# Attention probabilities moved into float32r tiles by a transfer before their transposes, with a reordered list of work for the attention stage

## The chip, the core and the metric

The kernel runs on one core of a Trainium2 chip. The metric is the device time in microseconds of one execution. The core has five engines that each work through their own instructions in order: TensorE (PE, matmuls and transposes), VectorE (DVE), ScalarE (ACT), GpSimd (POOL) and SyncE (SP), which here only issues transfers. Transfers are done by 16 DMA engines; SP, ACT and POOL each have a queue to issue them on. Engines wait for each other, and for transfers, through semaphores.

## The reference

A decoder trunk of two layers over 256 tokens of width 1024, in float32. Each layer is a SwiGLU FFN, a token mixer and a second FFN, each between RMS norms. The mixer of the first layer is a recurrent block, that of the second is attention with a forget gate. The change touches the attention alone:

```python
def forgetting_attention(xq, w_q, w_o, k, v, c):
    q = (xq @ w_q).reshape(Bn, S, N_HEADS, HEAD_DIM).transpose(0, 2, 1, 3) * (HEAD_DIM ** -0.5)
    for blk in range(S // Q_BLOCK):              # 2 blocks of 128 queries
        logits = einsum('bhqd,bhkd->bhqk', q[:, :, q0:end], k[:, :, :end])
        logits = logits + c[:, :, q0:end, None] - c[:, :, None, :end]
        logits = where(kpos[None, :] <= qpos[:, None], logits, -inf)
        p = softmax(logits, axis=-1)
        outs.append(einsum('bhqk,bhkd->bhqd', p, v[:, :, :end]))
    o = concatenate(outs, axis=2).transpose(0, 2, 1, 3).reshape(Bn, S, D_ATTN)
    return o @ w_o
```

There are 16 heads of 64. The first block of queries sees 128 keys, the second 256.

## The kernel before

**Tiles.** The 256 tokens are two tiles of 128, called tile 0 and tile 1 here (`t` in the code). Matmuls over weights are made at float32r speed with float32's accuracy: each weight block of 128x1024 is loaded by SP into a tile `raw` (ring of 5), ACT makes its upper part `whi` (L173), DVE the remainder `wlo` (L177), and `mm3` does three matmuls for each pair of operands: upper with upper (L183), upper with lower (L184), lower with upper (L185).

**Slots.** A weight block with the work on it is an item. One slot is one item's work for one tile: six matmuls of 128x512 in the attention stage, from `mm3`. Between slots, `tick` runs work that was put off by some slots (`defer`), such as the transposes of the q heads (L983) and of the next stage's inputs (L214).

**Order.** PE's instructions stand in the order in which the program writes them (`manual_schedule`). The other engines' order is made by the framework's scheduler, which knows the dependences and the parts marked as of high priority; once built it is fixed.

**The attention stage.** Its order of PE work is the list `ATT_ORDER`, read in L1367 to L1373. A `0` or `1` is the next slot of that tile: first eight for q (`attn_w_q`), then eight for the output product (`attn_w_o`, items 0 to 7, one for each 128 rows of W_o). Items 0 to 3 need the heads 0 to 7 of the attention's output, items 4 to 7 the heads 8 to 15. For tile 0 the last item's matmuls are made with its own slot, for tile 1 the last two items' are held back and made together in the last slot (`rows0=1`, `rows=2`). A letter with a tile's number is the next step of that kind of the tile's attention; groups are four heads for tile 0 (four groups, 0 to 3) and two heads for tile 1 (eight groups, 0 to 7), so that a group's probabilities are always 128x512:

- `l` (`logits`, L1097): logits of two groups at once, so every second `l` is empty: eight matmuls for tile 0 (128 keys), four for tile 1 (256 keys), into two banks. DVE adds the bias and takes the row's extreme (L1118) into a tile `pe` (ring of 3), makes the exponent's offset (L1122, L1123), ACT makes the exponentials with their row sums (L1125).
- `n` (`norm`, L1129): DVE's reciprocal of the row sums (L1131) and the product with them, in place in `pe` (L1132).
- `t` (`turn`, L1134): four transposes of `pe` on PE (L1138), in float32 with the float32 identity `ident`, and ACT's copy from the bank into `pT` (L1140, ring of 4).
- `v` (`values`, L1142): the products of `pT` with the values (L1152): four matmuls for each group. Behind the last group of each half of the heads, ACT and DVE write the upper and lower part of the output, `oh` (L1158) and `ol` (L1159), which are the left operands of the output product.

When a tile's output product is done, `enter` makes its row norm (ACT squares L205, POOL L198 and L200), adds it to the stream `h` (DVE L272, L285), and some slots later transposes `h` (L214) for the next FFN, whose left operands ACT (L223) and DVE (L222, L228) write.

**Elsewhere.** The FFN moves its hidden tile from float32 into a float32r tile `prr` by a transfer on SP's queue (L515), and transposes it as float32r with the float32r identity `identr` (L525). Its `prr` tiles, like several others, come from the tag `t1` of `hpool` (ring of 2).

Of the kernel before, what the change touches and what calls it, by code (L numbers as in the profile page):

```python
# [9 lines left out]
F32 = mybir.dt.float32  # L10
F32R = mybir.dt.float32r
# [5 lines left out]
P = 128  # L17
# [26 lines left out]
def trunk_kernel(ctx: ExitStack, tc: tile.TileContext, A: dict, out: bass.AP):  # L44
    nc = tc.nc
# [5 lines left out]
    hpool = ctx.enter_context(tc.tile_pool(name="h", bufs=1))  # L51
# [6 lines left out]
    def nm(s):  # L58
        uid[0] += 1
        return f"{s}_{uid[0]}"  # L60

    def mmbank():
        return psum.tile([P, 512], F32, tag="mm", name=nm("mm"), bufs=4)

    def gtbank():
        return psum.tile([P, 512], F32, tag="gt", name=nm("gt"), bufs=2)

    def trbank():
        return psum.tile([P, 512], F32, tag="tr", name=nm("tr"), bufs=2)
# [44 lines left out]
    ident = cpool.tile([P, P], F32, name="ident")  # L114
    make_identity(nc, ident)
    identr = cpool.tile([P, P], F32R, name="identr")
# [970 lines left out]
    def attention(t):  # L1087

        ap = pools["a"]
        nk = t + 1  # L1090
        per = 4 // nk
        bias = kv["bias0"] if t == 0 else att["bias1"]
        w = nk * P
        box = {}
        G = NH // per

        def logits(hg):  # L1097
            if hg % 2:
                return
            h0 = hg * per  # L1100
            ps = [gtbank() for _ in range(2)]

            def logit(hd):
                j = (hd - h0) // 2
                return ps[hd % 2][:, j * w:(j + 1) * w]

            for hd in range(h0, h0 + 2 * per):
                r = slice(hd % 2 * HD, (hd % 2 + 1) * HD)
                nc.tensor.matmul(logit(hd), att["q"][t][r, hd // 2, :], kv["kT"][r, hd // 2, :w], start=True, stop=True,
                                 skip_group_check=True)  # L1110
            if h0 % 8 == 0:
                box["sm"] = spool.tile([P, 8], F32, tag="sm", name=nm("sm"))
            for g in (hg, hg + 1):
                hds = range(g * per, (g + 1) * per)
                mx = spool.tile([P, 8], F32, tag="mx", name=nm("mx"))
                pe = ap.tile([P, per, w], F32, tag="pe", name=nm("pe"), bufs=3)
                for j, hd in enumerate(hds):
                    nc.vector.tensor_tensor_reduce(pe[:, j, :], logit(hd), bias[:, hd, :], -1.0, -NEG, ALU.add, ALU.min,  # L1118
                                                   mx[:, j:j + 1])
                cq = kv["cq"][t][:, h0 + (g - hg) * per:h0 + (g - hg) * per + per]  # L1120
                nm_q = mx[:, 4:]
                nc.vector.tensor_tensor(nm_q[:, :per], mx[:, :per], cq, ALU.add)  # L1122
                nc.vector.tensor_tensor(nm_q[:, :per], nm_q[:, :per], cq, ALU.subtract)  # L1123
                for j, hd in enumerate(hds):
                    nc.scalar.activation(pe[:, j, :], pe[:, j, :], AF.Exp, bias=nm_q[:, j:j + 1], scale=-1.0,  # L1125
                                         accum_out=box["sm"][:, hd % 8:hd % 8 + 1])
                box["pe", g], box["s", g] = pe, box["sm"][:, hds[0] % 8:hds[0] % 8 + per]

        def norm(hg):  # L1129
            pe, sm = box["pe", hg], box["s", hg]  # L1130
            nc.vector.reciprocal(sm, sm)  # L1131
            nc.vector.tensor_tensor(pe, pe, sm.unsqueeze(2).to_broadcast([P, per, nk * P]), ALU.mult)  # L1132

        def turn(hg):  # L1134
            tp = trbank()
            pev = box["pe", hg].rearrange("p a b -> p (a b)")
            for j in range(4):
                nc.tensor.transpose(tp[:, j * P:(j + 1) * P], pev[:, j * P:(j + 1) * P], ident)  # L1138
            pT = box["pT", hg] = ap.tile([P, 4, P], F32, tag="pT", name=nm("pT"), bufs=4)
            nc.scalar.activation(pT.rearrange("p a b -> p (a b)"), tp, AF.Copy)  # L1140

        def values(hg):  # L1142

            hds = range(hg * per, (hg + 1) * per)
            if hds[0] % 8 == 0:
                box["po"] = mmbank()
            po, pT = box["po"].rearrange("p (a b) -> p a b", a=4), box["pT", hg]
            for j in range(0, per, 2):
                for k in range(nk):
                    for s in range(2):  # L1150
                        hd = hds[j + s]
                        nc.tensor.matmul(po[s * HD:(s + 1) * HD, hd % 8 // 2, :], kv["v"][k][:, hd * HD:(hd + 1) * HD],  # L1152
                                         pT[:, (j + s) * nk + k, :], start=k == 0, stop=k == nk - 1)
            if hds[-1] % 8 == 7:
                b = hds[-1] // 8
                oh_v = att["oh"][t][:, 4 * b:4 * b + 4, :].rearrange("p a b -> p (a b)")
                ol_v = att["ol"][t][:, 4 * b:4 * b + 4, :].rearrange("p a b -> p (a b)")
                nc.scalar.activation(oh_v, box["po"], AF.Copy)  # L1158
                nc.vector.tensor_tensor(ol_v, box["po"], oh_v.bitcast(F32), ALU.subtract)  # L1159

        return {c: [lambda i=i, f=f: f(i) for i in range(G)] for c, f in zip("lntv", (logits, norm, turn, values))}

    def post_q(n):
        return lambda t, ps: heads_T(pools["a"], ps, t, n, HD ** -0.5, att["q"][t], "pT", 4)

    for n in range(2):
# [9 lines left out]
    ffn_items(lambda: pools["f"], A["ffn2_w_gate"][1], A["ffn2_w_up"][1], A["ffn2_w_down"][1], A["ffn2_post_g"][1],  # L1176
              lambda t: None, last=True)

    ATT_ORDER = ("0 0 0 0 0 0 0 l0 0 1 n0 l0 1 1 t0 n0 1 l0 v0 1 t0 n0 l0 1 v0 n0 1 t0 l1 1 v0 t0 n1 l1 0 v0 "
                 "n1 l1 t1 0 n1 l1 t1 0 n1 l1 v1 v1 t1 0 n1 l1 t1 0 n1 l1 v1 v1 t1 0 n1 l1 t1 0 n1 v1 v1 0 t1 1 "  # L1180
                 "t1 v1 1 v1 1 1 1 1 1 1")


    def half(t, i):
# [178 lines left out]
    att_rows()  # L1363

    steps = [attention(0), attention(1)]
    nxt = [n_ffn3, n_ffn3]
    for c in ATT_ORDER.split():  # L1367
        if c[0] in "lntv":
# [45 lines left out]
```

## Time and profile before

| | |
|---|---|
| median of 3 runs | 985.65 us (985.36 to 985.83) |
| the profiled execution's own time | 985.49 us |
| its span in the profile | 983.8 us |
| granted TensorE clock, mean | 0.998 |
| attention stage in the profile | about 735 to 785 us from the span's start |
| transfers, whole span | 196.71 MB, mean 200 GB/s |

Instructions are named by the line of the kernel that records them and by the tiles they write and read. A line of a timeline has the start (microseconds from the span's start), the duration, engine, line, operation, output and inputs, shapes and how many; in square brackets stand the idle time of the engine before it and what ended that. Durations of successive instructions overlap a little, since each engine's work is pipelined: the step from one start to the next is shorter than the duration.

### The profile page before, as it was taken

What the parts mean: (1) busy time and instruction counts of PE and PEld (TensorE: products, weight loads), DVE (VectorE), ACT (ScalarE), POOL (GpSimd) and SP (SyncE); (2) the same over time, 40 slices, a digit from 0 to 9 for tenths busy, and PEclk for the clock granted to TensorE, in tenths of its full rate; (3) what the DMA queues carried; (4) which work ended last, traced back from release to release, by engine and by line L of the source; (5) the groups of instructions that cost most, each with busy time, mean ns of one, the idle gap of its engine ahead of it and who ended that gap; (6) DMA issues with size and microseconds to landing.
All of it is one profiled execution on the core that took longest, in us unless ns stands there. A gap on an engine that the chain in (4) does not pass through costs nothing.

```text
span 983.8 us, 13107 instructions
## 1 busy us (share of the span) xinstructions
PE 975.3 (99%) x4783; PEld 808.8 (82%) x4783; DVE 610.6 (62%) x849; ACT 530.3 (54%) x753; POOL 58.2 (6%) x107
## 2 busy tenths in 40 slices
PE   9999999999999999999999999999999999999997
PEld 6888888898988888888898888888887788888886
DVE  6756554578997555554686555555487876555542
ACT  7545443568986544443565445444366855444431
POOL 2400000100002000000003000012020010000000
PEclk9999999999999999999999999999999999999999
DMA  8877766465346876666568877677672467766631
GB/s 284 282 255 244 225 214 187 155 202 161 111 122 211 235 214 205 217 210 192 132 191 285 235 203 222 212 236 228 214 262 77 131 204 235 213 213 213 205 117 43
DMA packets 100806, 196.71 MB, mean 200 GB/s; under 512 B 12894, under 2 KB 32710, under 8 KB 100614
## 3 DMA queue, kind: packets, MB, share of 16 engines
q1 hardware_dynamic: 98054, 188.95, 61.5%
q0 software_dynamic: 2080, 6.38, 2.2%
q8 instruction: 38, 0.62, 0.3%
q10 hardware_dynamic: 608, 0.53, 0.2%
q14 instruction: 26, 0.21, 0.1%
HBM read 182.19 MB, written 3.16 MB: 188 GB/s over the span
## 4 chain that ended last, share of the span: by engine, by line
PE 95%; DVE 2%; issue 1%; ACT 1%; DMA 0%; POOL 0%; POOLq 0%; ACTq 0%; DVEq 0%
PE mm L183 29%; PE mm L185 28%; PE mm L184 28%; PE gt L761 2%; PE tr L525 1%; PE mm L1249 1%; PE mm L190 1%; PE mm L191 1%; PE mm L192 1%; PE gt L214 1%; DVE wlo L177 1%; ACT pe L1125 0%; PE mm L1152 0%; DMA raw<-in_ffn_w_gate_dram 0%; DVE pe L1118 0%
## 5 line engine op out<-in xcount | busy, mean ns | idle before, releaser
L177 DVE TENSOR_TENSOR wlo<-raw,whi 128x1024 fp32r<-128x1024 f32 (+5 forms) x329 | 395.6, 1207 | 271.1 <-ACT whi L173 267.5
L173 ACT ACTIVATE whi<-raw 128x1024 fp32r<-128x1024 f32 (+5 forms) x329 | 342.0, 1046 | 313.0 <-PE mm L185 268.2
L183 PE MATMUL mm<-whi,xhi 128*128 128x512 f32 (+1 forms) x768 | 301.3, 392 | 0.0
L185 PE MATMUL mm<-whi,xlo 128*128 128x512 f32 (+1 forms) x768 | 298.2, 388 | 0.3 <-DVE xlo L228 0.3
L184 PE MATMUL mm<-wlo,xhi 128*128 128x512 f32 (+1 forms) x768 | 297.9, 388 | 0.0
L185 PEld LDWEIGHTS mm<-whi,xlo 128*128 128x128 f32 x768 | 144.2, 188 | 30.7 <-DVE xlo L228 0.7
L183 PEld LDWEIGHTS mm<-whi,xhi 128*128 128x128 f32 x768 | 144.2, 188 | 30.1 <-issue 2.0
L184 PEld LDWEIGHTS mm<-wlo,xhi 128*128 128x128 f32 x768 | 144.3, 188 | 28.3 <-DVE wlo L177 0.3
L183 PE MATMUL mm<-whi,hhi 128*128 128x512 f32 x352 | 137.8, 391 | 0.0
L185 PE MATMUL mm<-whi,hlo 128*128 128x512 f32 x352 | 137.0, 389 | 0.0
L184 PE MATMUL mm<-wlo,hhi 128*128 128x512 f32 x352 | 137.0, 389 | 0.0
L185 PEld LDWEIGHTS mm<-whi,hlo 128*128 128x128 f32 x352 | 66.1, 188 | 13.8
L183 PEld LDWEIGHTS mm<-whi,hhi 128*128 128x128 f32 x352 | 66.1, 188 | 13.5
L184 PEld LDWEIGHTS mm<-wlo,hhi 128*128 128x128 f32 x352 | 66.1, 188 | 13.2
L510 DVE SCALAR_TENSOR_TENSOR prod<-mm,rstd,sil 128x512 f32<-128x512 f32 (+1 forms) x48 | 33.9, 705 | 36.6 <-PE mm L185 32.3
L498 ACT ACTIVATE sil<-mm,rstd 128x512 f32<-128x512 f32 (+1 forms) x48 | 31.2, 653 | 41.2 <-PE mm L185 34.7
L198 POOL TENSOR_SCALAR nv<-ss 128x1 f32<-128x1 f32 x22 | 9.7, 441 | 558.1 <-ACT junk L205 558.1
L529 ACT ACTIVATE hhi<-tr 128x512 fp32r<-128x512 f32 (+1 forms) x48 | 24.8, 559 | 13.8 <-PE tr L525 13.8
L205 ACT ACTIVATE junk<-mm 128x512 bf16<-128x512 f32 x24 | 14.3, 595 | 32.4 <-PE mm L185 32.4
L530 DVE TENSOR_TENSOR hlo<-tr,hhi 128x512 fp32r<-128x512 f32 (+1 forms) x48 | 29.2, 641 | 2.6 <-ACT hhi L529 2.6
L272 DVE TENSOR_TENSOR t<-mm,gb 128x512 f32<-128x512 f32 x24 | 16.1, 685 | 23.6 <-ACT junk L205 23.4
L183 PE MATMUL mm<-whi,zhi 128*128 128x340 f32 (+2 forms) x80 | 28.2, 353 | 0.0
(203 smaller groups left out, 885.0 us busy)
## 6 DMA issues: line engine op xcount, KB each, us to landing
raw<-in_ffn_w_down_dram SPq DMA_DIRECT2D x88, 512.0 KB
raw<-in_ffn_w_up_dram SPq DMA_DIRECT2D x80, 512.0 KB
raw<-in_ffn_w_gate_dram SPq DMA_DIRECT2D x78, 512.0 KB
prr<-prod SPq DMA_DIRECT2D x40, 256.0 KB
raw<-in_rg_w_in_dram SPq DMA_DIRECT2D x10, 504.0 KB
raw<-in_rg_w_out_dram SPq DMA_DIRECT2D x10, 504.0 KB
raw<-in_ffn_w_gate_dram SPq DMA_DIRECT2D x19, 256.0 KB
raw<-in_ffn_w_up_dram SPq DMA_DIRECT2D x16, 256.0 KB
```

Of the source, the lines that this page charges most:

```text
L173: up = nc.scalar.activation(hi[:parts, c:c + m], rawv[:, c:c + m], AF.Copy)
L177: nc.vector.tensor_tensor(lo[:parts, c:c + m], rawv[:, c:c + m], hi[:parts, c:c + m].bitcast(F32), ALU.subtract)
L183: nc.tensor.matmul(ps, xh, wh, start=first, stop=False)
L184: nc.tensor.matmul(ps, xh, wl, start=False, stop=False)
L185: nc.tensor.matmul(ps, xl, wh, start=False, stop=last)
L205: nc.scalar.activation(junk[:, :src.shape[1]], src, AF.Square, scale=f, accum_out=acc)
L272: nc.vector.tensor_tensor(t1[n], pf[n], gb[:, n * 512:(n + 1) * 512], ALU.mult)
L498: nc.scalar.activation(s[:, :nn], ps, AF.Silu, scale=rs[t][:, 0:1])
L510: nc.vector.scalar_tensor_tensor(pr[:, :nn], ps, rs[t][:, 0:1], s, ALU.mult, ALU.mult)
L529: nc.scalar.activation(hv, tp[:, :nn], AF.Copy)
L530: nc.vector.tensor_tensor(lv, tp[:, :nn], hv.bitcast(F32), ALU.subtract)
L761: nc.tensor.matmul(ps[j][:w, g * S:(g + 1) * S], wv[rows, o:o + w], xc[rows, k, :], start=start, stop=stop, skip_group_check=True)
```

## The change

A `norm` now ends with a transfer on POOL's queue that copies the group's probabilities, bit for bit, from `pe` into a float32r tile of the same size. The tile comes from `t1` (ring of 2), for tile 1's last two groups from the tag `pT` (ring of 4). `turn` transposes that tile, as float32r and with `identr`. The list `ATT_ORDER` is another: the first step of each chain comes earlier, with more between a group's `n`, `t` and `v`; the numbers of slots and of steps are the same. Lines behind L1132 move by four, so that the transposes are L1142, the copy to `pT` L1144, the products with the values L1156, `oh` L1162 and `ol` L1163 in the changed kernel.

```diff
             nc.vector.tensor_tensor(pe, pe, sm.unsqueeze(2).to_broadcast([P, per, nk * P]), ALU.mult)
+            late = t == 1 and hg >= G - 2
+            moved = box["moved", hg] = (ap.tile([P, 512], F32R, tag="pT", name=nm("per"), bufs=4) if late else
+                                        hpool.tile([P, 512], F32R, tag="t1", name=nm("per"), bufs=2))
+            nc.gpsimd.dma_start(moved.bitcast(F32), pe.rearrange("p a b -> p (a b)"))
 
         def turn(hg):
             tp = trbank()
-            pev = box["pe", hg].rearrange("p a b -> p (a b)")
+            moved = box["moved", hg]
             for j in range(4):
-                nc.tensor.transpose(tp[:, j * P:(j + 1) * P], pev[:, j * P:(j + 1) * P], ident)
+                nc.tensor.transpose(tp[:, j * P:(j + 1) * P].bitcast(F32R), moved[:, j * P:(j + 1) * P], identr)
...
-    ATT_ORDER = ("0 0 0 0 0 0 0 l0 0 1 n0 l0 1 1 t0 n0 1 l0 v0 1 t0 n0 l0 1 v0 n0 1 t0 l1 1 v0 t0 n1 l1 0 v0 "
-                 "n1 l1 t1 0 n1 l1 t1 0 n1 l1 v1 v1 t1 0 n1 l1 t1 0 n1 l1 v1 v1 t1 0 n1 l1 t1 0 n1 v1 v1 0 t1 1 "
-                 "t1 v1 1 v1 1 1 1 1 1 1")
+    ATT_ORDER = ("0 0 0 0 0 0 0 l0 l0 0 1 n0 1 n0 1 l0 l0 1 t0 n0 1 t0 v0 n0 1 v0 l1 l1 t0 1 n1 t0 v0 1 n1 l1 l1 v0 0 "
+                 "t1 0 n1 t1 n1 0 l1 l1 v1 v1 0 t1 n1 0 t1 n1 l1 l1 v1 v1 0 t1 n1 0 t1 n1 0 v1 v1 1 1 t1 1 t1 1 v1 v1 "
+                 "1 1 1 1")
```

## The prediction

> **What bounds the kernel now.** I read the page first: how busy each engine is, then the chain of work that ended last.
>
> ```profile
> span 983.8 us, 13107 instructions
> ...
> PE 975.3 (99%) x4783; PEld 808.8 (82%) x4783; DVE 610.6 (62%) x849; ACT 530.3 (54%) x753; POOL 58.2 (6%) x107
> ...
> PE 95%; DVE 2%; issue 1%; ACT 1%; DMA 0%; POOL 0%; POOLq 0%; ACTq 0%; DVEq 0%
> ```
>
> TensorE (PE) works 99% of the span. Its order is written out by hand, so each microsecond that PE waits is a microsecond of the end, and work taken from PE is a gain of the same size. The table by stretches shows that this holds in the attention stage too, which runs from 735 to 785.
>
> ```profile
> 745.00:755.00 10.00, 10.00 (x73) 7.72 (x72) 8.60 (x36) 6.33 (x22) 0.00 (x0) 1.00 0.57 159
> 755.00:765.00 10.00, 10.00 (x71) 7.17 (x71) 6.74 (x30) 7.16 (x22) 0.00 (x0) 1.00 0.01 2
> 765.00:775.00 10.00, 10.00 (x78) 7.95 (x79) 10.00 (x31) 8.55 (x17) 0.00 (x0) 1.00 0.62 183
> 775.00:785.00 10.00, 9.92 (x68) 6.99 (x67) 7.65 (x15) 8.54 (x20) 1.65 (x4) 1.00 0.32 95
> ```
>
> The columns are PE, weight load, VectorE (DVE), ScalarE (ACT), GpSimd (POOL), granted clock, DMA share, GB/s. PE is full, and DVE (8.60 and 10.00 of 10) and ACT (8.54) nearly so: what moves work later on these two has little room. Among the waits of this window one touches PE's matmuls for lack of data, at 779.5; I count 0.5 us of waits in the stage before.
>
> ```profile
> PEld mm L183 <- DVE t L272: 0.5, 1, 0.5
> ```
>
> **The change, part by part.** First what PE gains. The chain of waits in order of time (start, us, what) prices PE's pieces:
>
> ```profile
> 742.85 0.44 PE tr L1138 x4
> ...
> 744.67 1.09 PE gt L1109 x16
> 745.76 0.59 PE mm L1152 x8
> 746.35 0.43 PE mm L183
> ...
> 827.99 0.63 PE tr L525 x8
> 828.62 0.30 PE mm L183
> 828.93 0.23 PE mm L184
> ```
>
> Four float32 transposes cost 0.44. Eight float32r ones (L525, the FFN's) cost 0.63, and the matmul behind them 0.30 for 0.23: 0.70, so 0.35 for four. Twelve turns times 0.09 give **-1.1 us**. A logits pair is 1.09 and 0.20 more on the next matmul (0.43 for 0.23): 1.29; a values step of tile 0 is 0.79; a slot, six matmuls, 1.38. The new list puts the attention pieces beside other neighbours, each meeting worth about 0.2 either way; laid out piece by piece it is 0.2 shorter. **PE: -1.3 us.**
>
> Now what the transfer adds. GpSimd issues twelve DMAs of 256 KB (128 rows of 2 KB, SBUF to SBUF); the engine is idle there (0.00 above; 1.65 in the last stretch, the row norm's) and SP's weight queue isn't touched. But a group's transposes can't start when its norm ends, they start when its transfer has landed, T later. Before, norm fed the transposes directly. No SBUF-to-SBUF transfer of POOL's queue stands in the trace, so T is bounded by the list of DMA issues (size, median to landing) and by the last line of the views of prow (0.3 and 4.9 KB rows) and bp (256 KB):
>
> ```profile
> bp<-crows POOLq DMA_DIRECT2D x4, 256.0 KB, 4.7
> prow<-in_rg_conv_w_dram POOLq DMA_DIRECT2D x4, 0.3 KB, 3.6
> DMA to landing us min/median/max: 2.8/4.8/5.7
> DMA to landing us min/median/max: 3.7/4.7/6.1
> ```
>
> Below, 2.8: even the smallest transfer took that. Above, 4.7: the median of 256 KB. The moved tile touches no DRAM and meets a DMA share of 0.01 to 0.62, so I place it between the shortest of each kind, 2.8 and 3.7: **T = 3.25**.
>
> [...]
>
> The list answers T by more distance between n (norm), t (turn) and v (values). To see if it suffices I laid out the changed order of each engine from 742.69 on, where the new PE order leaves the old (DVE: from 745.0), each instruction with duration and step of its row, started when engine and inputs are ready. The same layout of the old order ends within 0.1 us of the trace. Rows for it (DVE, ACT, PE):
>
> ```profile
> 741.09 0.69 DVE L1132 TENSOR_TENSOR pe<-pe,sm 128x512 f32<-128x512 f32 x1
> 742.90 0.18 DVE L1131 RECIPROCAL sm<-sm 128x4 f32<-128x4 f32 x1 [1.12 <-ACT pe L1125]
> 743.12 0.69 DVE L1132 TENSOR_TENSOR pe<-pe,sm 128x512 f32<-128x512 f32 x1
> ...
> 745.66 1.22 DVE L177 TENSOR_TENSOR wlo<-raw,whi 128x1024 fp32r<-128x1024 f32 x1
> 746.79 0.28 DVE L1118 CUSTOM_DVE_ANT_0 pe<-gt,bias 128x128 f32<-128x128 f32 x1
> ```
>
> ```profile
> 734.32 0.60 ACT L985 ACTIVATE qT<-tr 128x512 f32<-128x512 f32 x1 [1.94 <-PE tr L983]
> ...
> 739.60 0.39 ACT L1125 ACTIVATE pe<-pe,mx 128x128 f32<-128x128 f32 x1
> ...
> 778.64 0.60 ACT L205 ACTIVATE junk<-mm 128x512 bf16<-128x512 f32 x1
> ...
> 779.23 0.59 ACT L1140 ACTIVATE pT<-tr 128x512 f32<-128x512 f32 x1
> ```
>
> ```profile
> 733.64 0.60 PE L983 MATMUL tr<-ident,htok 128*128 128x128 f32 x4
> ```
>
> Tile 0, groups 0 to 3, T = 3.25 (0.24 from landing to the first matmul, which has its weight load ahead of it):
>
> - Group 0: norm ends 741.78, lands 745.0; PE arrives at 745.3. No wait.
> - Group 1: norm ends 743.81, lands 747.1; PE arrives 0.35 + 1.38 after t(0), at 747.0: **0.35**.
> - Group 2: behind norm 1 DVE has one L177 (step 1.13), eight bias steps of 0.21 for groups 2 and 3, one htok (0.66), small ones (0.4), two more L177 (2.26), then reciprocal and norm (0.9): 743.9 + 7.0, so norm 2 ends at 750.9 and lands at 754.1. PE arrives at 752.5: **1.9**. On the way the first logits of tile 1 wait **0.47** for the last q heads: transposes to ScalarE's copy 0.7 (733.64 to 734.32), copy 0.60 and weight load, against 1.0 of PE's work.
> - Group 3: its exponentials stand on ACT behind that q copy, the oh copy standing among them, at 0.38 each (751.2 to 753.3); reciprocal and norm behind a bias step end at 754.3; lands 757.6. Only one slot lies between t(2) and t(3): PE arrives at 756.1: **1.7**.
>
> Tile 1's transfers land 0.5 to 3.9 ahead of PE, but one 0.07 late. So the list's extra step covers eight of twelve transfers; behind T the late ones are norms that DVE and ACT reach late, and the bias steps that reuse a pe buffer (three of them) now wait for a landing. On POOL the row norm of tile 0's end (L198, L200) now stands behind the last two issues; its result is first needed by L214's transposes, four slots later, which covers it.
>
> Three waits come from the list itself, whatever T is:
>
> - In tile 0's last slot a wlo split stands on DVE behind the bias steps of the last groups: **0.75** (0 if DVE has caught up, 0.83 at most in my layouts).
> - v(5) of tile 1 stands one slot behind t(5), and that slot is tile 0's last. ACT does both L205 squares of tile 0's end before copying pT(5). Before, the second square began at 778.64, behind that slot's last matmul, and the pT copy ended at 779.82. PE has one values step (0.6) to do meanwhile, begun while that matmul still ran; with the weight load the layout leaves **1.2**.
> - Behind the last two values steps there are now four slots, before there were six. Rows 4 to 7 of W_o need the second half of oh and ol, so the next slot waits at once for oh (ACT) and then ol (DVE). Before, two slots of rows 2 and 3 covered it:
>
> ```profile
> 783.13 0.66 PE L1152 MATMUL mm<-pT,v 128*64 128x128 f32 x8
> 784.20 0.58 ACT L1158 ACTIVATE oh<-mm 128x512 fp32r<-128x512 f32 x1
> 785.47 0.68 DVE L1159 TENSOR_TENSOR ol<-mm,oh 128x512 fp32r<-128x512 f32 x1
> ```
>
> From this step's start to ol's end were 3.0 us (oh 1.65). With 0.24 for the load, oh holds PE for 1.1 and ol for 0.9 more; in my layout the next FFN's x copies stand in between: 1.28 and 1.22, together **2.5** (at least 1.4, with both engines free at once).
>
> Waits: 0.35 + 0.47 + 1.9 + 1.7 + 0.07 + 0.75 + 1.2 + 2.5 = 8.9. Less the 0.5 there before and less 1.3: **+7.1 us**. The profiled run took 985.49 (span 983.8 and 1.7 around it), 0.16 below the median of 985.65; 985.49 + 7.1 = **992.6 us**. Behind the stage the order is as before and PE-bound, so nothing is won back. Ends: T = 2.8 gives +6.35, T = 4.7 gives +12.0.
>
> **The rivals.**
>
> - Transfers at the median. T = 4.7: t(0) waits too, t(2) and t(3) 2.6 each, t(4) of tile 1 1.7; +12.0, 997.5. For it: both 256 KB kinds have 4.7. Against: both cross DRAM, under DMA load.
> - Transfers hidden. With T near 1 only 1.1 is left of the waits at t(2) and t(3), the list's own remain: +4.4, 989.9. For it: share 0.01 of the DMA engines in 755 to 765. Against: 2.8 for a few hundred bytes.
> - Faster: DVE and ACT run ahead. If the deeper list lets both reach norms, pT and oh some 2 us sooner than I lay out, every wait goes, and -1.3 - 0.5 is left: 983.7. It decides from the point where the sum of waits falls under 1.8. For it: DVE stands idle for 1.12 ahead of the norm at 742.90, waiting for an exponential that could come sooner. Against: oh and ol can't begin before the last values step ends, which alone costs 1.4.
> - The transposes don't get cheaper beside float32 matmuls: 1.1 lost, 993.7; inside my range.
>
> **How the numbers follow.** Forecast 0.62 (the last rival with it), its own range 990.5 to 995.5; median transfers 0.16; hidden ones 0.15; faster 0.03; between it and the hidden case, near zero change, 0.04. About 2 us (0.2%) is what a measurement here can tell from no change. So faster 0.03, same 0.04, slower 0.93. The range takes the hidden case in, and the median case with little above it: 989.0 to 998.0.
>
> **What would show it.** In the changed profile: L1142 transposes of four in 0.35; landings of the twelve transfers about 3.25 after their issue; PE idle of 1.5 to 2 ahead of the third and fourth turn, between 752 and 758, put down to DMA; about 1.2 ahead of an L1156 near 783 put down to ACT; two waits of over 1 near 793 put down to ACT L1162 and DVE L1163; none in the FFN behind. I am wrong if PE stays full from 750 to 760, if the end's two waits are missing, or if a landing takes over 4.5.

## The result, and the profile after

| | before | after |
|---|---|---|
| median (6 runs each) | 985.36 us (985.21 to 985.83) | 994.53 us (992.11 to 995.82) |
| ratio, 95% interval | | 1.0089 (1.0079 to 1.0100) |
| profiled execution, its span | 985.49 us, 983.8 us | 995.18 us, 993.4 us |

The changed kernel is slower by 9.2 us; 992.6 had been forecast. First, where the time was lost. The last float32r turn of the FFN ahead of the attention stage and the first behind it are the same work in both kernels. Their rows in the PE timeline (start, duration, engine, line, operation), before:

```profile
674.50 0.29 PE L525 MATMUL tr<-identr,prr 128*128 128x128 f32 x2
...
827.83 0.79 PE L525 MATMUL tr<-identr,prr 128*128 128x128 f32 x8
```

and after:

```profile
674.93 0.29 PE L525 MATMUL tr<-identr,prr 128*128 128x128 f32 x2
...
837.10 0.79 PE L525 MATMUL tr<-identr,prr 128*128 128x128 f32 x8
```

Between the two lie 153.33 us before and 162.17 after: **8.8 us are lost there**, 0.4 of the difference between the two profiled runs was there already when the stage began, and the last 0.4 came behind it. I use this stretch below, since it leaves out what differs from run to run ahead of the stage.

The same table by stretches that the prediction showed of before, now of after (PE, weight load, DVE, ACT, POOL, granted clock, DMA share, GB/s):

```profile
745.00:755.00 10.00, 7.32 (x53) 5.39 (x51) 8.41 (x35) 6.99 (x24) 0.91 (x3) 1.00 0.66 209
755.00:765.00 10.00, 8.99 (x50) 6.60 (x51) 5.55 (x21) 3.35 (x10) 1.58 (x3) 0.83 0.21 81
765.00:775.00 10.00, 10.00 (x71) 7.91 (x71) 7.02 (x25) 7.61 (x21) 1.08 (x2) 1.00 0.33 108
775.00:785.00 10.00, 8.76 (x67) 6.15 (x66) 9.31 (x24) 8.62 (x21) 2.15 (x4) 1.00 0.76 224
785.00:795.00 10.00, 8.50 (x56) 6.66 (x56) 6.58 (x9) 7.11 (x10) 1.65 (x4) 1.00 0.58 183
795.00:805.00 10.00, 8.69 (x37) 6.88 (x38) 7.60 (x10) 6.06 (x10) 1.32 (x2) 1.00 0.64 198
```

PE, full in these stretches before but for 0.08 in one, now has holes in all but one; and in 755 to 765 the granted clock is 0.83. The view of waits of PE between 735 and 810 names them (sum, times, longest):

```profile
PE tr L1142 <- DMA per<-pe: 4.7, 2, 3.6
PE mm L185 <- DVE ol L1163: 1.0, 1, 1.0
PE mm L1156 <- ACT pT L1144: 1.0, 1, 1.0
PE mm L183 <- ACT oh L1162: 0.7, 1, 0.7
PE mm L184 <- DVE wlo L177: 0.2, 1, 0.2
```

Of these 7.6 us, 4.7 are waiting for two of the twelve transfers and 2.9 for ScalarE and VectorE. The third turn of tile 0 in the PE timeline, with the hole ahead of it and what follows:

```profile
751.28 1.14 PE L1109 MATMUL gt<-kT,qT 64*128 64x256 f32 x8
756.01 0.51 PE L1142 MATMUL tr<-identr,per 128*128 128x128 f32 x4 [3.59 <-DMA per<-pe]
...
757.70 0.63 PE L185 MATMUL mm<-whi,xlo 128*128 128x512 f32 x1
758.12 0.67 PE L1142 MATMUL tr<-identr,per 128*128 128x128 f32 x4
758.72 1.12 PE L1156 MATMUL mm<-pT,v 128*64 128x128 f32 x8
```

Two things are to be seen. The idle time is 3.59, twice the 1.9 forecast. And from 757.7 the instructions last longer: L185 0.63 for its usual 0.39, a values step 1.12 for 0.66. That is the granted clock at half (0.50 from 757.45 to 760.86). The next two stretches of 5 us show it:

```profile
755.00:760.00 5.00, 3.99 (x23) 3.09 (x24) 2.81 (x10) 2.75 (x9) 1.04 (x2) 0.74 0.15 57
760.00:765.00 5.00, 5.00 (x28) 3.51 (x29) 2.74 (x11) 0.60 (x1) 0.54 (x1) 0.91 0.27 105
```

0.26 x 5 and 0.09 x 5 are 1.75 us of lost clock. The prediction has no such term.

### The profile page after: what moved, and what is told of

Its sections match the earlier page's. It is cut to its first block, busy times and chain, and to the rows that moved or that the text cites. A ratio compares the mean times of both kernels' runs of the same rounds, so it can differ in the third digit from the quotient of the medians.

```text
span 993.4 us, 13151 instructions
## 1 busy us (share of the span) xinstructions
PE 977.5 (98%) x4783; PEld 809.5 (81%) x4783; DVE 611.0 (62%) x849; ACT 530.6 (53%) x753; POOL 65.0 (7%) x119
## 5 line engine op out<-in xcount | busy, mean ns | idle before, releaser
L183 PE MATMUL mm<-whi,xhi 128*128 128x512 f32 (+1 forms) x768 | 301.6, 393 | 0.0
L185 PE MATMUL mm<-whi,xlo 128*128 128x512 f32 (+1 forms) x768 | 298.5, 389 | 0.3 <-DVE xlo L228 0.3
L185 PEld LDWEIGHTS mm<-whi,xlo 128*128 128x128 f32 x768 | 144.4, 188 | 30.8 <-DVE xlo L228 0.7
L183 PEld LDWEIGHTS mm<-whi,xhi 128*128 128x128 f32 x768 | 144.3, 188 | 30.2 <-issue 1.8
L183 PE MATMUL mm<-whi,hhi 128*128 128x512 f32 x352 | 137.8, 392 | 0.0
L185 PE MATMUL mm<-whi,hlo 128*128 128x512 f32 x352 | 137.1, 389 | 0.0
L185 PEld LDWEIGHTS mm<-whi,hlo 128*128 128x128 f32 x352 | 66.1, 188 | 13.8
L183 PEld LDWEIGHTS mm<-whi,hhi 128*128 128x128 f32 x352 | 66.1, 188 | 13.4
L205 ACT ACTIVATE junk<-mm 128x512 bf16<-128x512 f32 x24 | 14.3, 594 | 32.9 <-PE mm L185 32.9
L272 DVE TENSOR_TENSOR t<-mm,gb 128x512 f32<-128x512 f32 x24 | 16.1, 686 | 23.5 <-ACT junk L205 23.4
L183 PE MATMUL mm<-whi,zhi 128*128 128x340 f32 (+2 forms) x80 | 28.2, 353 | 0.0
```

The costliest lines, as they stand in the source:

```text
L183: nc.tensor.matmul(ps, xh, wh, start=first, stop=False)
L185: nc.tensor.matmul(ps, xl, wh, start=False, stop=last)
L205: nc.scalar.activation(junk[:, :src.shape[1]], src, AF.Square, scale=f, accum_out=acc)
L272: nc.vector.tensor_tensor(t1[n], pf[n], gb[:, n * 512:(n + 1) * 512], ALU.mult)
```

## The experiments

All times stand beside runs of the kernel before on the same chip. "Stretch" is the time between the two L525 rows above, less the 153.33 of before; "falls" counts the places from 735 to 805 with a granted clock at half. Both are of the one profiled run, whose own time can lie off the median: 994.97 in e8_mended, 996.99 in e2_old_list, 984.83 in e10_norm_later.

| run | edit, in short | median us | ratio, 95% interval | stretch us | falls |
|---|---|---|---|---|---|
| after | the change | 994.53 | 1.0079 to 1.0100 | +8.8 | 1 |
| e1_list_alone | new list, nothing else | 990.33 | 1.0027 to 1.0054 | +4.8 | 1 |
| e2_old_list | transfers, old list | 998.00 | 1.0109 to 1.0137 | +11.5 | 2 |
| e4_fill | PE kept busy in the long wait | 993.64 | 1.0062 to 1.0089 | +7.9 | 0 |
| e5_tail | one more slot at the end | 993.80 | 1.0070 to 1.0113 | +8.0 | 1 |
| e8_mended | list mended in three places | 992.20 | 1.0059 to 1.0084 | +8.8 | 2 |
| e11_mended_fill | the same, PE kept busy in two waits | 990.10 | 1.0035 to 1.0060 | +3.9 | 0 |
| e3_direct_r | float32r without transfer, ring of two | 985.72 | 0.9997 to 1.0015 | +0.4 | 0 |
| e7_direct_ring | the same, ring of four | 985.40 | 0.9991 to 1.0009 | 0.0 | 0 |
| e10_norm_later | the same, last norm later | 985.43 | 0.9989 to 1.0007 | -0.3 | 0 |

Two kernels that ran once each, e6_load (998.78) and e9_load2 (994.37), ask about the transfers and stand at the end.

**The list alone.** The kernel before with the new list:

```diff
-    ATT_ORDER = ("0 0 0 0 0 0 0 l0 0 1 n0 l0 1 1 t0 n0 1 l0 v0 ...
+    ATT_ORDER = ("0 0 0 0 0 0 0 l0 l0 0 1 n0 1 n0 1 l0 l0 1 t0 ...
```

> The kernel before with the new ATT_ORDER alone: no transfer, float32 transposes. Theory (the list costs time by itself: q heads' copy, the wlo split in tile 0's last slot, v(5) of tile 1 behind the two L205 squares, oh and ol at the end): the waits the changed kernel shows at these places, 0.3 + 0.5 + 1.0 + 2.4 = 4.2, less 0.5 present before, less 0.2 of regrouping: +3.5, about 988.9 us (2.7 by laying the order out with the trace's durations, 988.1); no wait ahead of any turn, granted clock 1.00 in every stretch from 735 to 800. Rival (all the loss comes from the transfers): 985.4, within 0.5.

Measured 990.33, in four runs 990.37, 990.47, 988.52 and 990.28. The waits of PE:

```profile
PE mm L183 <- ACT oh L1158: 1.4, 1, 1.4
PE mm L185 <- DVE ol L1159: 0.9, 1, 0.9
PE mm L1152 <- ACT pT L1140: 0.6, 1, 0.6
PE gt L1109 <- ACT qT L985: 0.2, 1, 0.2
```

The list loses 4.8 us of the stretch without a single transfer: oh, ol, pT and qT, as said, the wlo split not. But the clock fell here too, which was not expected, behind the waits for oh and ol:

```profile
789.57 0.50 PE L183 MATMUL mm<-whi,oh 128*128 128x512 f32 x1 [1.41 <-ACT oh L1158]
...
791.16 0.80 PE L185 MATMUL mm<-whi,ol 128*128 128x512 f32 x1 [0.86 <-DVE ol L1159]
```

```profile
790.00:795.00 5.00, 4.14 (x12) 3.04 (x11) 1.75 (x3) 1.06 (x1) 0.00 (x0) 0.66 0.44 133
```

0.34 x 5 are 1.7 us; without them the list costs 3.1, and one of the four runs, 988.52, stood at that (its mean granted clock was 0.998, that of the other three 0.997). The rival, that transfers make all of the loss, falls.

**The transfers with the old list.** The reverse: the changed kernel with the old `ATT_ORDER`.

> The changed kernel with the old ATT_ORDER: transfers and float32r transposes, norms one step nearer to their turns. Theory (norm's end to landing is 2.9 us where SP's weight loads are quiet and 3.5 to 5.6 where they run; the old list leaves less than that between n and t): waits ahead of most turns, +6.6 if all twelve take 2.9, +17.4 if all take 4.7, less by more than one turn's wait if a wait lets later landings catch up; I take +10, 995.5, so no better than the new list, with the waits at per<-pe instead of at oh and ol. The end's oh and ol waits are gone. [...] Rival (the transfers are hidden, only the list costs): 984.3, faster than before by the 1.1 of the transposes.

Measured 998.0 (996.99 to 999.23). The waits of PE:

```profile
PE tr L1142 <- DMA per<-pe: 9.3, 5, 3.9
```

Nothing but landings, five of twelve; oh and ol are gone. The time is 2.5 above the forecast, which had no fall of the clock in it. Behind two of these waits, one of 3.91 and one of only 2.03, the clock fell:

```profile
745.00:750.00 5.00, 5.00 (x34) 3.63 (x33) 3.64 (x12) 0.84 (x2) 0.00 (x0) 0.69 0.94 306
...
780.00:785.00 5.00, 2.74 (x9) 2.33 (x10) 2.75 (x11) 1.57 (x5) 0.54 (x1) 0.72 0.55 189
```

So the new list is worth 2.7 us of the stretch to a kernel with transfers (11.5 against 8.8; 3.5 by the medians), and costs one without them 3.1 to 4.8.

**The clock.** Fourteen matmuls of constants in the long wait of the changed kernel:

```diff
         def turn(hg):
             tp = trbank()
             moved = box["moved", hg]
+            if t == 0 and hg == 2:
+                for _ in range(14):
+                    nc.tensor.matmul(tp, nc.const_aps.tensor(1.0, (P, P), BF16), nc.const_aps.tensor(1.0, (P, 512), BF16),
+                                     start=True, stop=True)
```

> The changed kernel, with 14 matmuls of bfloat16 constants (128x512, about 0.2 us each) on TensorE ahead of the transposes of group 2 of tile 0, into the bank that the transposes then overwrite. They run in the 3.6 us in which TensorE waits for that group's landing. Theory (the idle stretch of 3.6 us is what brought the granted clock down to 0.74 in 755 to 760 and 0.91 in 760 to 765, which costs 0.26 x 5 + 0.09 x 5 = 1.75 us): clock 1.00 in both stretches, time 1.0 to 2.5 below the changed kernel's 994.5, about 992.8, and a smaller spread over its runs. Rival (the clock falls for another reason, such as the power drawn by this stretch or the time since launch): the same fall, 994.5 within 0.7; or, if the matmuls hold up the turn, more.

Measured 993.64, five runs from 992.99 to 993.68, 0.7 apart where the changed kernel's six lay 3.7 apart. The clock stayed up:

```profile
755.00:760.00 5.00, 3.97 (x28) 3.12 (x28) 2.72 (x10) 2.11 (x7) 1.07 (x2) 1.00 0.27 105
760.00:765.00 5.00, 5.00 (x34) 3.61 (x33) 3.16 (x14) 1.47 (x4) 0.00 (x0) 1.00 0.14 52
```

The cause is shown: it was the idle stretch. The other runs agree, as far as their mean clocks tell: the changed kernel's six took 995.82 and 995.68 at 0.995, 995.18 at 0.996, 993.89 and 993.28 at 0.997, and 992.11 at 0.999, while these five all had 0.998 or 0.999. The gain is 0.9, in the stretch and in the medians (whose intervals overlap), just under the 1.0 to 2.5 expected, since a PE at full speed now waits there for the pT copy:

```profile
PE mm L1160 <- ACT pT L1148: 1.6, 2, 1.0
```

(Lines behind L1139 stand four higher in this run.) The changed kernel had one such wait, of 1.0; the new one of 0.6 takes part of the 1.75 back.

**The end.** One slot moved behind the last values steps:

```diff
-                 "... 0 v1 v1 1 1 t1 1 t1 1 v1 v1 1 1 1 1"
+                 "... 0 v1 v1 1 1 t1 t1 1 v1 v1 1 1 1 1 1"
```

> The changed kernel with the list's tail '1 1 t1 1 t1 1 v1 v1 1 1 1 1' written as '1 1 t1 t1 1 v1 v1 1 1 1 1 1': one slot of W_o more behind the last values steps, so that a slot of rows that need only the first half of oh and ol stands there. Theory (the end's two waits of 1.2 each are oh and ol coming late): the oh wait is gone and 1.0 of the ol wait is left, t(7) comes up to 1 us before its landing at 789.5 only if t(6) no longer waits: 1.0 to 1.4 below the changed kernel, 993.3. Rival (both engines are simply behind, and the wait moves to the next place): 994.5 within 0.7, with the same 2.4 of waits at oh and ol or at whi and wlo.

Measured 993.80 in the middle of four runs (one at 998.72); that is too coarse to tell it from 994.53. The waits can:

```profile
PE tr L1142 <- DMA per<-pe: 4.3, 2, 3.4
PE mm L185 <- DVE ol L1163: 1.1, 1, 1.1
```

oh is gone and 1.1 of ol is left, as the theory had it, and the stretch is 0.9 shorter, a little under the 1.0 to 1.4 expected.

**The list mended.** Three edits at once, each at one of the waits:

```diff
-  v0 l1 l1 t0 1 n1 t0 v0 1 n1 l1 l1 v0 0
+  v0 l1 l1 1 t0 n1 1 t0 v0 n1 l1 l1 v0 0
...
-  0 v1 v1 1 1 t1 1 t1 1 v1 v1 1 1 1 1
+  0 1 v1 v1 1 t1 t1 1 v1 v1 1 1 1 1 1
```

> The changed kernel with its list mended at three places: the slot behind the third turn of tile 0 stands ahead of it, one of the slots ahead of v(5) of tile 1's pair stands between it and tile 0's last slot, and the last two turns stand together with one slot more behind the last values steps. Theory (the loss is the sum of single waits at named places, each worth what stands on the page, plus the granted clock's fall behind the longest): the third turn's wait falls from 3.6 to 2.2 or less and the clock stays at 1.00, the pT wait of 1.0 and the oh wait of 1.2 go: 4.5 by laying the order out, 1 more for the clock: 989 to 990. What is left above before is landings. Rival (the waits only move on to the next late landing, as the fourth turn's did behind the third's): 993 to 994.5.

Measured 992.2 (990.8 to 994.97), 2 to 3 above the forecast. The waits for pT, oh and ol at the places mended are gone (0.5 for L272 is new), but the waits put down to landings still add up to 4.7, as in the changed kernel, now in four places for two. So for the landings the rival held: their waits moved on. The clock fell behind the two long ones:

```profile
755.87 0.68 PE L1142 MATMUL tr<-identr,per 128*128 128x128 f32 x4 [1.93 <-DMA per<-pe]
...
789.16 1.23 PE L1142 MATMUL tr<-identr,per 128*128 128x128 f32 x8 [2.27 <-DMA per<-pe]
```

I had expected a wait of 2.2 or less to leave the clock alone. The 1.93 did not in this run. The other four runs had mean clocks of 0.997 to 0.999 for its 0.996, so they hold fewer falls. The next run keeps PE busy in both waits (eight matmuls of constants at each, written as in e4_fill):

> The run e8_mended with 8 bfloat16 matmuls of constants (1.8 us) ahead of the transposes of group 2 of tile 0 and of group 6 of tile 1, where TensorE waited 1.9 and 2.3 for the landings and the granted clock then fell to 0.50 for some 3.4 us each time (990 to 995 us, with clock 0.999 to 0.996). Theory (idle stretches of about 2 us in a row already bring the clock down, each fall costing 1.7 us): clock 1.00 in every stretch from 735 to 805, all runs within 1 us of the best of e8_mended, 990.8. Rival (the falls are not caused by these two waits): clock 0.83 in 755 to 765 or 785 to 795 again, and 992.2 within 1.

Measured 990.1 (989.25 to 991.13), the clock 1.00 in every stretch, the stretch 3.9 above before for 8.8. The theory holds: the clock stays up, and two of the five runs came out even lower than forecast. Of the 4.9 between the two profiled runs the two falls are 3.4; the other 1.5 was not traced. In the medians the gain is 2.1. What is left is mostly landings, now under the filling matmuls (twice 1.8 us).

**Float32r without a transfer.** The norm writes into float32r tiles itself; the list is that of before.

```diff
-            nc.vector.tensor_tensor(pe, pe, sm.unsqueeze(2).to_broadcast([P, per, nk * P]), ALU.mult)
+            late = t == 1 and hg >= G - 2
+            moved = box["moved", hg] = (ap.tile([P, 512], F32R, tag="pT", name=nm("per"), bufs=4) if late else
+                                        hpool.tile([P, 512], F32R, tag="t1", name=nm("per"), bufs=2))
+            nc.vector.tensor_tensor(moved.rearrange("p (a b) -> p a b", a=per), pe,
+                                    sm.unsqueeze(2).to_broadcast([P, per, nk * P]), ALU.mult)
```

> The kernel before, with its old ATT_ORDER and no transfer: the norm on VectorE writes the probabilities straight into the float32r tiles (rounded to that type as they are written), and they are transposed as float32r. Theory (the type alone gives TensorE 0.09 per turn, and without a transfer the old list has nothing to wait for): twelve times 0.09, 1.1 below before, 984.4, at least 0.5; four L1142 transposes and the change-over in 0.35; the norm as long as before, 0.69. Rival (the transposes are no cheaper here, or ScalarE and VectorE hold the stage): 985.4 within 0.2.

Measured 985.72: no gain. PE waited 0.8 for a norm and 0.4 for a wlo split. I put it down to the ring of two, and took all twelve tiles from the ring of four (`tag="pT"`):

> The run e3_direct_r with its float32r tiles taken from the ring of four that the pT tiles use, instead of the ring of two. In e3_direct_r the transposes were cheaper, but TensorE waited 0.8 for a norm that stood behind four wlo splits on VectorE (770.7 to 771.9) and 0.4 for a wlo; before, that norm stood between those splits. Theory (the ring of two moved that norm back, and the 1.2 it cost hid the gain of 1.1): with four tiles the two waits go and the gain shows, 984.0 to 984.4 (laying the order out: 1.45 below before). Rival (VectorE, busy 10.00 of 10 from 765 to 775, bounds this stretch whatever the order, so that each 0.1 saved on TensorE there is waited for): 985.4 to 985.7.

Measured 985.40: no gain again, though both waits had gone. The rival was right. This is PE and DVE at the end of tile 0 in e7_direct_ring (here the transposes are L1140, the norm L1133):

```profile
777.59 0.46 PE L1140 MATMUL tr<-identr,per 128*128 128x128 f32 x4
...
779.73 0.50 PE L183 MATMUL mm<-whi,oh 128*128 128x512 f32 x1 [0.91 <-DVE t L272]
```

```profile
776.73 0.16 DVE L1123 TENSOR_TENSOR mx<-mx,cq 128x2 f32<-128x2 f32 x1
778.11 0.17 DVE L1131 RECIPROCAL sm<-sm 128x2 f32<-128x2 f32 x1 [1.22 <-ACT pe L1125]
778.38 0.69 DVE L1133 TENSOR_TENSOR per<-pe,sm 128x512 fp32r<-128x512 f32 x1
778.99 1.28 DVE L272 TENSOR_TENSOR t<-mm,gb 128x512 f32<-128x512 f32 x2
```

and the same place before:

```profile
778.24 0.60 PE L1138 MATMUL tr<-ident,pe 128*128 128x128 f32 x4
...
779.62 0.50 PE L183 MATMUL mm<-whi,oh 128*128 128x512 f32 x1
```

Ten turns had gained PE 0.65 (777.59 for 778.24), and at the next L183 nothing of it was left (779.73 for 779.62). That matmul waits for L272 to empty its bank; L272 stands on DVE behind a norm, the norm behind an exponential, that behind DVE's own L1123, and DVE had worked without a break until that L1123 from 764.2 on (before shows the same, 10.00 of 10 from 765 to 775 in the prediction's row). So this chain seems to set the time here, before too, where PE's 0.5 of waiting stood. A last try took the norm out of the way:

```diff
-  t1 0 n1 v1 v1 0 t1 1 t1 v1 1 v1 1 1 1 1 1 1
+  t1 0 v1 v1 0 t1 n1 1 t1 v1 1 v1 1 1 1 1 1 1
```

> The run e7_direct_ring with the last norm of tile 1 one step later in the list (behind tile 0's last slot and the turn of group 6), so that VectorE does the first L272 of tile 0's end ahead of that norm. In e7_direct_ring TensorE was 0.65 ahead of before at that point (L1140 at 777.59 against L1138 at 778.24) and then waited 0.91 there for L272, which stood behind the norm of group 7, itself waiting 1.22 for the last exponential; before waited 0.5 at the same place. Theory (the chain from the exponentials over norm and L272 sets the time there, and takes the transposes' gain away): L272's first half comes 0.7 earlier, the wait falls to 0.2, and the gain is kept: 984.7, within 0.4. Rival (the next thing on VectorE, L272's second half or the wlo splits behind, holds TensorE as long): 985.4 within 0.2.

Measured 985.43. The profiled run shows the stretch 0.3 shorter than before, which the medians don't. L272 now started 0.6 sooner, and waited for something else:

```profile
778.40 0.69 DVE L272 TENSOR_TENSOR t<-mm,gb 128x512 f32<-128x512 f32 x1 [0.41 <-ACT junk L205]
```

ScalarE's square of the same bank (L205), itself behind the exponentials. So it is not one norm that holds PE here: with that out of the way, the next step of the two engines does. No version was found that is faster than the kernel before.

**What a landing depends on.** Each transfer's time from issue to landing in the changed kernel, one view for each window: 2.2 to 2.4 for seven of the twelve, 2.8 and 3.2 for two, 4.1 for the third (issued at 751.79) and 5.1 for the last two (783.79 and 784.42). The slowest meet SP's weight loads: 257 GB/s moved in 750 to 755 and 221 in 780 to 785, against 57 in 755 to 760. Counted by queue, SP's packets alone moved 151 GB/s during the landing of 4.1 and 98 to 140 during those of 5.1, but at most 45 during the seven quick ones. The fit is not perfect: the landing of 2.8 had 160 beside it, that of 3.2 none, and no run shows why. To try this, SP was given traffic where there was none:

```diff
             nc.gpsimd.dma_start(moved.bitcast(F32), pe.rearrange("p a b -> p (a b)"))
+            if t == 1 and hg == 0:
+                nc.sync.dma_start(spare[0], pe.rearrange("p a b -> p (a b)"))
+                nc.sync.dma_start(spare[1], A["w_kv"][:, :512])
```

> The changed kernel; behind the norm of group 0 of tile 1, SP's queue copies that group's probabilities (256 KB) and 2 MB of w_kv to scratch DRAM tiles that nothing reads. In the changed kernel this group's transfer and the next (issued at 759.2 and 760.2, no weight load running) landed 2.3 us after issue. Theory (a transfer lands late because SP's traffic shares the DMA engines with it: 4.1 and 5.1 while weights came at 210 to 260 GB/s): these two now take 4 us or more, the first ones of tile 0 stay at 2.3 to 2.4. Rival (the late landings come from GpSimd's queue or from how the issue is fed, not from the load): 2.3 again. Time: t of these groups comes 3.5 and 4.6 us behind the landings in the changed kernel, so that alone costs nothing; the copies may hold up SP's next weight loads, 994.5 to 999.

This missed its aim: the 2 MB waited for nothing, so they were issued 13 us into the kernel, and only the 256 KB came at 761.5. The two landings took 2.3 as ever: 256 KB of other traffic, begun half a microsecond ahead, did not delay them. (Of the 13.4 by which its one time of 998.78 lies above before, 2.8 were there ahead of the stage, the 2 MB at the start being the likely cause; and the clock, at 0.79 in 755 to 760 and 0.53 in 760 to 765, stayed down twice as long as elsewhere.) With the order of the two pinned:

> The changed kernel; behind the norm of group 0 of tile 1, SP's queue copies that group's probabilities (256 KB) and, right behind, 2 MB of w_kv to scratch DRAM tiles that nothing reads; unlike e6_load, where the 2 MB went out at 13 us, at the kernel's start, they now stand behind the first copy. Theory (SP's traffic delays a transfer): the second transfer of tile 1, issued about 1 us after the first, lands 3.5 us or more after its issue instead of 2.3; the first, whose data moves before, 2.3 to 3. Rival (late landings come from GpSimd's queue or issue): 2.3 for both. Time 994.5 to 999, the later weight loads of SP standing behind the copies.

The first transfer, by the view of the tiles in the window of its issue (min/median/max, of one):

```profile
DMA to landing us min/median/max: 3.6/3.6/3.6
```

the second by the same view of the window of its own,

```profile
DMA to landing us min/median/max: 7.1/7.1/7.1
```

and what moved in those 5 us:

```profile
760.00:765.00 5.00, 5.00 (x33) 3.57 (x32) 3.15 (x14) 0.78 (x2) 0.11 (x1) 0.96 0.86 278
```

3.6 (2.3 to 3 had been expected) and 7.1, where both had been 2.3: here traffic on SP's queue delayed them. That the weight loads did it to the late landings of the changed kernel rests on their meeting in time. The time stayed at 994.37, since these two groups have slack.

## Why the prediction came out right, and where it didn't

The direction and the size held, and so did the kinds of wait: late landings, and waits of the list's own. Where the landings would be late held for one place of four. 992.6 was 1.9 short of 994.53. Step by step:

| step | forecast | found in the profile of after |
|---|---|---|
| third turn of tile 0 | 1.9 | 3.6 |
| fourth turn of tile 0 | 1.7 | none |
| second turn; fifth turn | 0.35; 0.07 | none |
| seventh turn of tile 1 | none | 1.25 |
| q heads' copy | 0.47 | 0.1 |
| wlo split | 0.75 | 0.46 |
| v(5) behind L205 | 1.2 | 1.1 |
| oh and ol at the end | 2.5 | 1.9 |
| sum of waits | 8.9 | 8.4 |
| fall of the clock | none | 1.4 to 1.75 |
| transposes, regrouping | -1.1, -0.2 | -0.7, not measured apart |
| there before | -0.5 | -0.25 to -0.5 |

The right column is from start to start in the PE timeline, less the step of the work between, good to about 0.1 a place. With the middle of each range it adds up to 8.4 + 1.6 - 0.7 - 0.4 = 8.9; the stretch is 8.8 longer.

**T.** One T of 3.25 for all twelve was the mis-sized term. The prediction took it from rows that count from a transfer's issue, and laid it from the norm's end; the way from there to the issue on POOL was put at nothing. DVE's norm and POOL's issue of the third group:

```profile
750.46 0.69 DVE L1132 TENSOR_TENSOR pe<-pe,sm 128x512 f32<-128x512 f32 x1
```

```profile
751.79 0.54 POOL L1136 DMA_DIRECT2D per<-pe  x1 [6.45 <-ACT pe L1125]
```

The norm ends at 751.15, 0.25 later than laid out; POOL begins 0.64 after that (0.56 to 0.64 for the eleven whose issue had no other issue ahead of it); the transfer lands 4.1 later. From the norm's end that is 4.7 here and 2.9 where SP is quiet, so 3.25 lay between two cases and was neither; the 0.6 left out and the 0.95 by which 3.25 lies above a quiet landing of 2.3 cancel in part. 1.9 + 0.25 + (4.7 - 3.25) is the 3.6 measured. The fourth turn's wait went because PE came to it two microseconds late: its norm ended at 754.32, as laid out, and the transfer landed at 757.2, 0.4 sooner, but PE came at 758.12. The two waits together are 3.6, forecast and found: that the sum came out right though its parts did not is luck, and so is that the seventh turn's 1.25 stands in for waits that were absent. The prediction called itself wrong if a landing took over 4.5. Two did (5.1), and one of them is the 1.25 of the seventh turn, a wait that the layout had not.

**The clock** was left out: 1.4 to 1.75 in the profiled run, 0.9 in e4_fill, which shows the cause, as e11_mended_fill does again; so it is half or more of the 1.9 by which the forecast was short. The one run of the six at a mean clock of 0.999 took 992.11, beside the 992.6 forecast.

**The list's own waits** were right: e1_list_alone has them without any transfer, at 3.1 plus a fall of the clock, and e5_tail takes away the one at oh. In the changed kernel they start as forecast:

```profile
784.28 0.66 PE L1156 MATMUL mm<-pT,v 128*64 128x128 f32 x8 [1.01 <-ACT pT L1144]
...
795.28 0.50 PE L183 MATMUL mm<-whi,oh 128*128 128x512 f32 x1 [0.70 <-ACT oh L1162]
...
797.04 0.50 PE L185 MATMUL mm<-whi,ol 128*128 128x512 f32 x1 [1.03 <-DVE ol L1163]
```

**"Work taken from PE is a gain of the same size"** was a step that failed. The transposes got cheaper, though by 0.06 a turn and not 0.09 (0.65 ahead of before, of which 0.08 was there at the stage's start, over ten turns). But with the old list the gain was worth nothing (e3, e7, e10): PE at 10.00 of 10 had hidden that DVE, also at 10.00, and ACT behind it were just as late at the end of tile 0. Whether the changed kernel keeps the 0.7 among its waits was not tried by itself.

**The rivals.** Transfers at the median of 4.7: near it or above were three landings (4.1, 5.1, 5.1), not twelve. Hidden: the 4.7 of waits for landings speak against it, and 9.3 with the old list; e1_list_alone, which has no transfers, stands at 990.33, where this rival stood (its terms add up to +4.2, not the +4.4 written). Faster: it needed waits of under 1.8, and they were 8.4. Transposes no cheaper: they are.

## What to carry to other kernels

A transfer put into a chain need not have one latency: the same copy of 256 KB took from 2.2 to 5.1 us to land in the changed kernel, and 7.1 in e9_load2. Price it by what the other queues move at that very time, and look at which transfers fall beside loads before choosing where the list gives distance. An engine that shows 99% busy is not the only bound; before crediting time taken from it, look for the next engine whose step it nearly waits for, here the 0.5 at L272. And where a trace shows the granted clock fall behind an idle stretch of TensorE, count that stretch twice: here once as the wait (1.93 to 3.91 us, where it was a single one), and once as the 1.7 us that the half-speed clock lost.

## What the runs showed of the hardware

The granted clock fell to half for 3.4 us, of which 1.7 are lost, behind idle stretches of TensorE of 3.59 (after), 3.91 and 2.03 (e2_old_list), 1.93 and 2.27 (e8_mended), and behind 1.41 and 0.86 that lay 0.7 us apart (e1_list_alone). In e6_load it was 6.8 us, at a wait of 3.9. It did not fall behind 0.70 and 1.03 as near to each other (after), nor behind single ones of 1.30 and 1.18 (e2_old_list).

Cut into stretches of the fall's own length, 3.41 us, the time around the fall of after reads (PE's busy time comes first behind the length, the granted clock is the third number from the end):

```profile
750.62:754.03 3.41, 1.70 (x16) 1.01 (x16) 2.42 (x9) 2.61 (x10) 0.54 (x1) 1.00 0.88 320
754.03:757.45 3.42, 1.44 (x9) 1.29 (x10) 1.47 (x8) 1.50 (x5) 0.54 (x1) 1.00 0.31 119
757.45:760.86 3.41, 3.41 (x18) 2.47 (x17) 1.72 (x4) 1.77 (x7) 1.08 (x2) 0.50 0.17 66
```

and in e1_list_alone, ahead of its fall at 790.87:

```profile
787.46:790.87 3.41, 1.44 (x16) 0.76 (x12) 3.41 (x6) 2.06 (x4) 0.55 (x1) 1.00 0.97 314
```

The wait of 3.59 lies across the first two of these stretches, with 1.71 us of idle time in one and 1.98 in the next, and the fall came 1.4 us after the wait had ended. In e1_list_alone its two waits, neither over 1.41, put 1.97 into the 3.41 us ahead of the fall. So in these two runs the fall did not go by the length of a single wait alone. How much idle time it takes, and over what time, was not shown.

A transfer of 256 KB within SBUF on GpSimd's queue took 2.2 to 2.4 us from issue to landing in seven of twelve cases, with at most 45 GB/s on SP's queue, and up to 7.1 us beside 2 MB on SP's queue.
